# Longer runs of transposes and fewer switches to the attention products, in a hybrid attention and state-space layer

## The chip, the cores and the metric

The kernel runs on one core of one Trainium2 chip. The metric is device time in microseconds (us), the median of three runs. The profile is one further execution; its times are counted from its first instruction.

The engines are named as the profile names them: PE is TensorE (PEld its weight loads), DVE VectorE, ACT ScalarE, POOL GpSimd, SP the queue that issues most of the DMAs.

## The reference

One layer of a decoder trunk, for one sequence of 1024 tokens with 1024 channels, in float32:

```python
mod = c_act @ w_ada[layer] + b_ada[layer]
shift, scale, gate = jnp.split(mod, 3, axis=-1)
h = rms_norm(x, norm_in_gain[layer]) * (1.0 + scale[:, None, :]) + shift[:, None, :]
proj = h @ w_in[layer]
q, k, v, z_attn, xbc, dt_raw, z_ssm = jnp.split(proj, splits, axis=-1)
# stick-breaking attention, 16 heads of 64, in blocks of 128 queries:
z = jnp.einsum("bqhd,bkhd->bhqk", q[:, start:end], k[:, :end]).astype(jnp.float32) * scale
log_one_minus = jnp.where(mask, jax.nn.log_sigmoid(-z), 0.0)
tail = lax.cumsum(log_one_minus, axis=3, reverse=True) - log_one_minus
weights = jnp.exp(jnp.where(mask, log_beta + tail, -jnp.inf))
outs.append(jnp.einsum("bhqk,bkhd->bqhd", weights.astype(v.dtype), v[:, :end]))
# beside it a Mamba-2 head group (16 heads of 64, chunks of 128) on silu(conv(xbc))
y_attn = rms_norm(o, sb_norm_gain[layer]) * jax.nn.silu(z_attn)
y_ssm = rms_norm(y * jax.nn.silu(z_ssm), ssm_norm_gain[layer])
mixed = jnp.concatenate([y_attn, y_ssm], axis=-1) @ w_out[layer]
x = x + gate[:, None, :] * mixed
return rms_norm(x, norm_f_gain)
```

## The kernel before, in words

Every large projection is made of three products of float32r parts (high by high, high by low, low by high), 128x128 weights against 512 columns, summed in one PSUM bank. Splitting a weight piece into its two parts costs DVE (and, early, ACT).

**Front** (lines 424 to 630, up to some 80 us). x, the modulation weights and the first projection weights are loaded. `norm_x` (442) squares a row block on ACT, takes a root on ACT, a reciprocal on DVE, and scales the block on DVE. `ada_mm`, `ada_sum` and `ada_turn` make shift and scale in four rounds from a product on PE and sums on DVE. `turn_x` and `modulate` (500) transpose x on PE and make the high and low parts of h; `mm_h` (517) is the first projection. `fillers` (545) are products with the identity whose result is not used. This stage is in an order written out by hand, on all engines.

**State-space group** (633 to 1220, up to some 315 us): its order is a planner's.

**Attention** (from 1222, some 315 to 940 us): again an order by hand. Heads go in eight pairs. `ROUND` (931) lists the steps of a pair: `scores` (937, "s": PE products of q and k into four banks of `pz`, then sigmoids on ACT, scans and weights on DVE, spread out by `tick`), `turned` (997, "t": the weights of one block of 128 queries are transposed on PE four 128x128 blocks at a time into the single bank of `pt`, and ACT copies the bank back over the weights), and `values` (1013, "v": PE products with v for two blocks, into the single bank of `pv`). The two heads of a pair share PE: scores use half of its rows for each head, values half of its columns. Between these steps `fill` (1285) puts "sides" (`SIDES`, 1189): the projections of q, k, v and the gates for later pairs (`inproj_f`, 295; `inproj_v`, 312), the last one with `turn` (1072), and for pair 7 the state-space half of the output projection (`out_ssm`, 1142). A side gives one step at a time, mostly three matmuls of 512 columns (0.7 us); its sum stands in the two banks of `pj` by turns, and its evacuation (`evac`) reads the bank on ACT (q, k, v) or on ACT and then DVE (gates: `zgate_evac`, 912, `gate_ssm`, 799; output: 1152). `fill(..., True)` after four transposes makes at least one side step, except near a pair's end.

**Tail** (1319 to 1402): the rest of the output projection, in one stretch on PE.

Of the kernel before, what the change touches and what calls it, by code (L numbers as in the profile page):

```python
# [14 lines left out]
P = 128  # L15
# [11 lines left out]
def hybrid_layer_kernel(  # L27
# [156 lines left out]

    h_hi, h_lo = [None] * KT, [None] * KT
# [109 lines left out]
    def inproj_f(col, evac, between=None):  # L295


        wts = take(2) if pinned[0] else split_f(load_f(col))
        for b in range(2):
            ps = bank(pj, "pj")  # L300
            for k in range(KT):
                mm_f(ps, wts, k, b)
                if pinned[0]:
                    ahead()
                    if b and k % 4 == 3:
                        used()
                yield 0.7
            evac(b, ps)
            if between:
                yield between(b)  # L310

    def inproj_v(vc, with_dt, v_tiles, dt_raw, extra=None):
# [19 lines left out]
        for i in range(TB):  # L332
            ps = bank(pj, "pj")
            ts_ = slice(i * P, (i + 1) * P)
            for k in range(KT):
                whi, wlo, ws = wts[k]
                K(T.matmul(ps[:, :n], h_hi[k][:, ts_], whi[:, ws], start=(k == 0), stop=False))  # L337
                K(T.matmul(ps[:, :n], h_hi[k][:, ts_], wlo[:, ws], start=False, stop=False))  # L338
                if i == 0 and extra:
                    extra(ps[:, n:n + TB], k)  # L340
                K(T.matmul(ps[:, :n], h_lo[k][:, ts_], whi[:, ws], start=False, stop=(k == KT - 1)))  # L341
                if not with_dt:
                    ahead()
                    if i == TB - 1 and k % 2:
                        used()
                if k == 3:
                    yield 1.4
            if i == 0 and extra:
                extra(ps[:, n:n + TB], KT)
            for j in range(2):  # L350
                A.copy(v_tiles[j][:, i * P:(i + 1) * P], ps[:, j * P:(j + 1) * P])
            if with_dt:
                A.copy(dt_raw[:, i, :], ps[:, 256:272])
            yield 1.4
# [54 lines left out]
    def split_w4(k):  # L409
# [9 lines left out]
        A.copy(w_hi[k], w_raw[k])  # L419
# [22 lines left out]
    def norm_x(i):  # L442
        junk = mk(op, "om", [P, 1028], bufs=2)
        A.activation(junk[:, :S], xt[i], AF.Square, accum_out=ssq[:, i:i + 1])
        A.activation(rstd[:, i:i + 1], ssq[:, i:i + 1], AF.Sqrt, scale=1.0 / D, bias=eps_t[:, 0:1])
        V.reciprocal(rstd[:, i:i + 1], rstd[:, i:i + 1])
        V.tensor_scalar_mul(xt[i], xt[i], rstd[:, i:i + 1])
# [52 lines left out]
    def modulate(k, hb, ptt=None, c0=0, c1=HALF, full_v=False):  # L500
        ptt = turn_x(k, hb) if ptt is None else ptt
# [11 lines left out]
        V.tensor_tensor(h_lo[k][:, sl], hf, h_hi[k][:, sl].bitcast(F32), op=ALU.subtract)  # L513

    us = []
# [76 lines left out]
    for c_ in range(1, 4):  # L592
# [8 lines left out]
        if c_ == 3:  # L601
            split_lo(6)
        ada_add(c_, ada_turn(c_))
        mm_h(k + 1, 0, range(cut, 4), *cs)
        if c_ < 3:
            ada_mm(c_ + 1)

            mid = (0, 0, 1, 3)[c_ + 1]
            ada_sum(c_ + 1, range(4, 4 + mid - 1), False)
            split_lo(k + 2), split_lo(k + 3)  # L610
# [12 lines left out]
    modulate(1, 1, full_v=True)  # L623
# [175 lines left out]
    def gate_ssm(j):  # L799
# [10 lines left out]
        yield from inproj_f(C_ZS + j * P, evac)  # L810
# [111 lines left out]
    def zgate(p):  # L922
        yield from inproj_f(C_Z + p * P, zgate_evac(p))
# [10 lines left out]
    tiles, pav = {}, {}  # L934
    seq = {"made": 0, "scanned": [], "weights": set()}

    def scores(p, g):
# [5 lines left out]
        for i in {i for i, _, _ in GROUPS[g]}:  # L943
            if i % 2 == 1:
                tiles[p, i // 2] = [duo(), duo()]
        oms = [mk(op, "om", [P, 1028], bufs=2), mk(sp, "bc", [P, S], bufs=4)]
        parts = []
        for i, c0, cw_ in GROUPS[g]:
            zs = [bank(pz, "pz") for _ in range(2)]
            mw = max(cw_, 256)  # L950

            for n, (a, k_) in enumerate(((qh, kh), (qh, kl), (ql, kh))):
                for e in range(2):
                    r = slice(64 * e, 64 * e + 64)
                    K(T.matmul(zs[e][:, :mw], a[r, i * P:(i + 1) * P], k_[r, c0:c0 + mw],  # L955
                               start=(n == 0), stop=(n == 2)))
            parts.append((i, c0, cw_, zs))
        off = {}
        for i, _, _, _ in parts:
            off.setdefault(i, 0 if i == g else 512)  # L960

        def sigmoids(i, c0, cw_, z, e):
            W = (i + 1) * P
            last = c0 + cw_ == W
            be, om = tiles[p, i // 2][e][:, i % 2], oms[e][:, off[i] + c0:off[i] + c0 + cw_]
# [16 lines left out]
        def weights(i, e):  # L982
            W = (i + 1) * P
            be, om = tiles[p, i // 2][e][:, i % 2], oms[e][:, off[i]:off[i] + W]
# [12 lines left out]
    def turned(p, i):  # L997

        for e in range(2):
            if (p, i, e) not in seq["weights"]:  # L1000
                flush("A", lambda: (p, i, e) in seq["weights"] or not late["A"])
                flush("V", lambda: (p, i, e) in seq["weights"])
            be = tiles[p, i // 2][e][:, i % 2]
            for j0 in range(0, i + 1, 4):
                j1 = min(i + 1, j0 + 4)
                ptt = bank(pt, "pt")
                for j in range(j0, j1):
                    K(T.transpose(ptt[:, (j - j0) * P:(j - j0 + 1) * P], be[:, j * P:(j + 1) * P], ident))  # L1008
                A.copy(be[:, j0 * P:j1 * P], ptt[:, :(j1 - j0) * P])
                tick(0.11 * (j1 - j0))  # L1010
                fill(0.5 + 0.1 * (j1 - j0), True)

    def values(p, i0):
        tl, hb, q0 = tiles.pop((p, i0 // 2)), i0 // 4, i0 % 4
        if q0 == 2:
            pav[p] = bank(pv, "pv")
        for j in range(i0 + 2):
            u = int(j > i0)
            for e in range(2):
                K(T.matmul(pav[p][64 * e:64 * e + 64, (q0 + u) * P:(q0 + 2) * P],  # L1020
                           vs[p][:, j * P + 64 * e:j * P + 64 * e + 64],
                           tl[e][:, u:2, j * P:(j + 1) * P], start=(j == 0), stop=(j > i0)))
        if q0 == 2:
            return
# [6 lines left out]
        else:  # L1031
            sq = mk(sp, "th", [P, S], bufs=1)
            A.activation(sq[:, sl], pav[p], AF.Square)
            V.tensor_tensor(sq_a[:, sl], sq_a[:, sl], sq[:, sl], op=ALU.add)
        V.tensor_tensor(zgs[p][:, sl], pav[p], zgs[p][:, sl], op=ALU.mult)
        if hb == 0:
            after(3.0, lambda: (SP.dma_start(y_d[p], zgs[p]), stored.add(p)))
        tick(0.2 * i0 + 0.4)


    def gate_row(b):
        gate = row["sum"][:, b * HALF:(b + 1) * HALF]
        pg = bank(pj, "pj")
# [4 lines left out]
    def outproj(w_h, w_l, evac, first=None):  # L1048

        yt = take(2)  # L1050
        for b in range(2):
            ps = first if first is not None and b == 0 else bank(pj, "pj")
            sl = slice(b * HALF, (b + 1) * HALF)
            for k in range(KT):
# [5 lines left out]
                if b and k % 4 == 3:  # L1060
                    used()
                yield 0.7
            evac(sl, ps)
# [8 lines left out]
    def turn():  # L1072


        wts = take(2)
        pss = [bank(pj, "pj") for _ in range(2)]
# [57 lines left out]
        RATE["V"] = 0.8  # L1134

# [6 lines left out]
    def out_ssm():  # L1142
# [6 lines left out]
        for i in range(TB):  # L1149
            t3 = []  # L1150

            def evac(sl, ps):
                if not t3:
# [37 lines left out]
    COST = {"z": 11.2, "g": 11.2, "q": 22.4, "v": 22.4, "t": 11.3, "o": 36.0}  # L1191
# [42 lines left out]

    def side_step():
# [4 lines left out]
    def count(what, i):  # L1240
        if what == "s":
            return 4.0
        if what == "v":
# [24 lines left out]
    def back(k):  # L1268
# [12 lines left out]
        for n in range(2):  # L1281
            after(2.0, lambda n=n: load_a(k + n, raw[:, n]))
            after(8.0 + 2.0 * n, lambda n=n: split_a(k + n, lambda: place(n)))
# [9 lines left out]
    for p in range(9):  # L1293
        for what, i, before in ROUND:
# [4 lines left out]
            elif what == "t":  # L1299
                turned(p + before, i)  # L1300
            else:
                while p not in box:
                    side_step()
                scores(p, i)
                fill(4.0)
            if (p, what, i) == (6, "s", 1):
# [7 lines left out]
            if (p, what, i) == (7, "s", 1):  # L1314
                front()
            if p == 8 and what == "v":
                back(4 if i else 6)
# [113 lines left out]
```

## Time and profile before

| | us |
|---|---|
| median of 3 runs | 1072.83 (1072.72 to 1073.05) |
| the profiled execution | 1072.53 |
| its span, first to last instruction | 1070.8 |
| PE busy | 1052.9 (98%) |
| DVE busy | 766.2 (72%) |
| ACT busy | 535.6 (50%) |

The busy time of PE counts an instruction from its start to its modelled end, and matmuls overlap, so what PE loses between two kinds of work stands in the distances of the starts rather than as idle time. A float32 matmul stands in the profile as two instructions, one for each pass.

### The profile page before, as it was taken

What the parts mean: (1) busy time and instruction counts of PE and PEld (TensorE: products, weight loads), DVE (VectorE), ACT (ScalarE), POOL (GpSimd) and SP (SyncE); (2) the same over time, 40 slices, a digit from 0 to 9 for tenths busy, and PEclk for the clock granted to TensorE, in tenths of its full rate; (3) what the DMA queues carried; (4) which work ended last, traced back from release to release, by engine and by line L of the source; (5) the groups of instructions that cost most, each with busy time, mean ns of one, the idle gap of its engine ahead of it and who ended that gap; (6) DMA issues with size and microseconds to landing.
All of it is one profiled execution on the core that took longest, in us unless ns stands there. A gap on an engine that the chain in (4) does not pass through costs nothing.

```text
span 1070.8 us, 16251 instructions
## 1 busy us (share of the span) xinstructions
PE 1052.9 (98%) x6323; PEld 836.3 (78%) x6323; DVE 766.2 (72%) x1333; ACT 535.6 (50%) x1163; POOL 2.9 (0%) x23
## 2 busy tenths in 40 slices
PE   7999999999999999999999999999999999999997
PEld 5789887777878777798777887778876777688886
DVE  4838879988848765844977658969387789664554
ACT  5655497676433454554645446546465664420111
POOL 0000000000000000000000000000000000000000
PEclk9999999999999999999999999999999999999999
DMA  9610332233202220201321102311011522555432
GB/s 349 225 41 23 99 107 85 70 96 128 70 20 60 89 78 22 60 20 40 89 60 40 50 21 79 79 40 41 21 50 50 187 88 90 193 186 195 165 108 78
DMA packets 91559, 96.14 MB, mean 90 GB/s; under 512 B 5998, under 2 KB 75994, under 8 KB 91484
## 3 DMA queue, kind: packets, MB, share of 16 engines
q1 hardware_dynamic: 88828, 86.45, 25.8%
q10 hardware_dynamic: 2656, 8.67, 2.3%
q8 instruction: 49, 0.80, 0.3%
q14 instruction: 26, 0.21, 0.1%
HBM read 78.26 MB, written 16.84 MB: 89 GB/s over the span
## 4 chain that ended last, share of the span: by engine, by line
PE 96%; ACT 1%; DMA 1%; DVE 1%; issue 0%; SPq 0%; DVEq 0%; ACTq 0%
PE pj L292 41%; PE pj L1058 15%; PE pt L1008 7%; PE pv L1020 6%; PE pz L955 6%; PE pz L528 4%; PE pj L337 3%; PE pj L341 3%; PE pj L338 3%; PE pz L774 2%; PE pv L788 1%; PE pz L779 1%; PE pj L1380 1%; PE pz L761 1%; PE pj L1123 1%; PE pz L1058 1%
## 5 line engine op out<-in xcount | busy, mean ns | idle before, releaser
L292 PE MATMUL pj<-hh,whi 128*128 128x512 f32 x544 | 225.9, 415 | 0.3 <-ACT th L62 0.3
L292 PE MATMUL pj<-hh,wlo 128*128 128x512 f32 x544 | 214.5, 394 | 0.0
L292 PE MATMUL pj<-hl,whi 128*128 128x512 f32 x544 | 212.7, 391 | 0.0
L62 ACT COPY be<-pt 128x512 f32<-128x512 f32 (+1 forms) x192 | 92.4, 481 | 136.7 <-PE pt L1008 134.4
L292 PEld LDWEIGHTS pj<-hh,whi 128*128 128x128 f32 x544 | 102.5, 188 | 25.3 <-issue 6.3
L292 PEld LDWEIGHTS pj<-hh,wlo 128*128 128x128 f32 x544 | 102.1, 188 | 22.9 <-issue 0.7
L292 PEld LDWEIGHTS pj<-hl,whi 128*128 128x128 f32 x544 | 102.7, 189 | 16.8 <-issue 0.5
L62 ACT ACTIVATE be<-pz 128x512 f32<-128x512 f32 (+3 forms) x192 | 100.9, 526 | 0.0
L1008 PE MATMUL pt<-ident,be 128*128 128x128 f32 x576 | 97.6, 278 | 1.8 <-ACT be L62 1.6
L1008 PEld LDWEIGHTS pt<-ident,be 128*128 128x128 f32 x576 | 67.6, 140 | 38.6 <-ACT be L62 29.0
L62 DVE TENSOR_TENSOR wlo<-raw,whi 128x512 fp32r<-128x512 f32 (+1 forms) x109 | 75.3, 691 | 22.9 <-ACT whi L62 15.9
L62 ACT ACTIVATE om<-pz 128x512 f32<-128x512 f32 (+2 forms) x96 | 47.5, 495 | 75.6 <-PE pz L955 74.8
L62 DVE TENSOR_TENSOR_SCAN om<-om,ident 128x128 f32<-128x128 f32 x64 | 26.8, 419 | 65.9 <-ACT om L62 65.6
L62 DVE TENSOR_TENSOR_SCAN om<-om 128x896 f32<-128x896 f32 (+6 forms) x56 | 71.9, 1285 | 2.0
L62 DVE TENSOR_TENSOR_SCAN bc<-bc 128x896 f32<-128x896 f32 (+6 forms) x56 | 71.9, 1285 | 2.0
L1020 PE MATMUL pv<-be,v 128*64 128x256 f32 (+1 forms) x640 | 69.3, 363 | 0.0
L62 DVE TENSOR_TENSOR be<-be,bc 128x1023 f32<-128x1023 f32 (+4 forms) x78 | 65.3, 838 | 2.4
L337 PE MATMUL pj<-whi,hh 128*128 128x256 f32 (+1 forms) x224 | 66.4, 296 | 0.0
L1020 PEld LDWEIGHTS pv<-be,v 128*64 128x64 f32 x640 | 43.1, 136 | 28.7 <-issue 8.3
L955 PE MATMUL pz<-big,big 64*128 64x384 f32 (+2 forms) x576 | 65.3, 357 | 0.2 <-DVE big L62 0.2
L341 PE MATMUL pj<-whi,hl 128*128 128x256 f32 (+1 forms) x224 | 64.4, 288 | 0.0
L338 PE MATMUL pj<-wlo,hh 128*128 128x256 f32 (+1 forms) x224 | 63.6, 284 | 0.0
(287 smaller groups left out, 1988.4 us busy)
## 6 DMA issues: line engine op xcount, KB each, us to landing
raw<-in_w_in_dram SPq DMA_DIRECT2D x98, 256.0 KB, 2.8
be<-acT_d ACTq DMA_DIRECT2D x16, 512.0 KB, 3.9
big<-in_x_dram SPq DMA_DIRECT2D x10, 512.0 KB, 4.6
aw<-in_w_ada_dram SPq DMA_DIRECT2D x16, 256.0 KB, 5.6
u_d<-big SPq DMA_DIRECT2D x8, 512.0 KB, 3.1
y_d<-bc SPq DMA_DIRECT2D x8, 512.0 KB, 2.6
raw<-in_w_ada_dram SPq DMA_DIRECT2D x16, 256.0 KB, 2.6
raw<-u_d SPq DMA_DIRECT2D x16, 256.0 KB, 2.8
```

The source lines that it names most:

```text
L62: return lambda *args, **kw: K(op(*args, **kw))
L292: K(T.matmul(ps, w[:, ws], h[:, b * HALF:(b + 1) * HALF], start=(k == 0 and n == 0), stop=(k == KT - 1 and n == 2)))
L337: K(T.matmul(ps[:, :n], h_hi[k][:, ts_], whi[:, ws], start=(k == 0), stop=False))
L338: K(T.matmul(ps[:, :n], h_hi[k][:, ts_], wlo[:, ws], start=False, stop=False))
L341: K(T.matmul(ps[:, :n], h_lo[k][:, ts_], whi[:, ws], start=False, stop=(k == KT - 1)))
L528: K(T.matmul(acc[f][:, c0:c1], w[:, f * P:(f + 1) * P], h[:, sl], start=(k == 0 and n == 0 and c0 == 0), stop=(k == KT - 1 and n == 2)))
L761: K(T.transpose(px[:, j * P:(j + 1) * P], xs[4 * g + j][:, ts_], ident))
L774: K(T.matmul(po, xd[:, 0, h, :], m[:, h, :], start=True, stop=(ch == 0)))
L955: K(T.matmul(zs[e][:, :mw], a[r, i * P:(i + 1) * P], k_[r, c0:c0 + mw], start=(n == 0), stop=(n == 2)))
L1008: K(T.transpose(ptt[:, (j - j0) * P:(j - j0 + 1) * P], be[:, j * P:(j + 1) * P], ident))
L1020: K(T.matmul(pav[p][64 * e:64 * e + 64, (q0 + u) * P:(q0 + 2) * P], vs[p][:, j * P + 64 * e:j * P + 64 * e + 64], tl[e][:, u:2, j * P:(j + ...
L1058: K(T.matmul(ps, y[:, ks], w(k, b), start=(k == 0 and n == 0), stop=(k == KT - 1 and n == 2)))
```

## The change

What it does, in six parts:

1. `turned` takes up to two banks of transposes in one run (up to eight 128x128 blocks), the first in `pt`, the second in one of the two `pj` banks; where four blocks or fewer are left for both heads, both go into one bank. Before a run of more than four blocks it makes side steps until the running projection has between 1.3 and 3.6 us left (2.2 where `slow` is set, for projections that DVE evacuates), by `left`, which each side now keeps. While `turn` holds both `pj` banks, a run has one bank.
2. `values` come in two runs a pair instead of four: blocks 6 and 4 one behind the other, 2 and 0 one behind the other. The score group of blocks 1 and 0 is gone; block 1 goes with block 5 and block 0 with block 4, in banks that these leave half empty. So a pair has five score groups, not six. The matmuls are the same, but for the cut of block 5.
3. Blocks 2 and 3 have tiles of their own (`bs`); blocks 1 and 0 lie in the tiles of 5 and 4.
4. The front: the norms are cut into parts and interleaved anew, more of `modulate` is on DVE, one split moves to DVE, three fillers go, `split_lo` comes ahead of `ada_add`, and the loads of x blocks 4 to 7 come ahead of the seven small tables (`late_loads`).
5. `gate_row` uses `pt`, not `pj`; the output projection's `evac` is written ahead of its last `yield`; in `values` the product with the gate comes ahead of the sum of squares.
6. The order near the end: pair 7's first scores wait in the order for the first bank of the output projection; `front`, `back` and the cost of side "o" are set anew; `dynamic_dma_scratch_size=8192`.

The diff, cut:

```diff
-    def inproj_f(col, evac, between=None):
+    def inproj_f(col, evac, between=None, by_v=False):
...
+                left[0], slow[0] = 0.7 * (KT - 1 - k), by_v
                 yield 0.7
...
     load_w4(6), load_w4(7)
-    late_loads()
     for i in range(4, TB):
         load_x(i)
+    late_loads()
...
     fillers(3)
+    norm_sq(1)
+    split_w4(0, V)
+    norm_rt(1)
     pa = ada_turn(0)
-    norm_x(1)
+    norm_by(1, 0, 256)
     ada_add(0, pa)
+    fillers(1)
+    turn_pair(1)
     fillers(4)
-    turn_pair(1)
-    split_w4(0)
-    norm_x(2)
+    norm_sq(2)
...
     split_lo(0)
-    modulate(0, 0, pts[0], *half[0])
+    norm_by(1, 256)
+    modulate(0, 0, pts[0], *half[0], full_v=True)
+    norm_rt(2)
     split_w4(1)
     split_lo(1)
-    modulate(1, 0, pts[1], *half[0])
-    fillers(4)
+    modulate(1, 0, pts[1], *half[0], full_v=True)
+    norm_by(2, 0, 256)
+    norm_sq(3), norm_rt(3)
+    norm_by(3, 0, 256)
     mm_h(0, 0, range(4), *half[0])
+    mm_h(1, 0, range(4), *half[0])
     turn_pair(2)
-    mm_h(1, 0, range(4), *half[0])
-    norm_x(3)
+    turn_pair(3)
     ada_mm(1)
-    turn_pair(3)
+    norm_by(2, 256), norm_by(3, 256)
...
-    norm_x(4)
-    modulate(6, 0, pts[0], full_v=True)
-    split_lo(7)
-    modulate(7, 0, pts[1], full_v=True)
-    norm_x(5), norm_x(6), norm_x(7)
+    norm_sq(4), norm_rt(4), norm_sq(5), norm_rt(5)
+    for f in (h_full, h_low):
+        f(6, 0, pts[0]), f(7, 0, pts[1])
+        if f is h_full:
+            norm_by(4), norm_by(5)
+            split_lo(7)
+    norm_sq(6), norm_rt(6), norm_sq(7), norm_rt(7)
+    norm_by(6, 0, 256), norm_by(7, 0, 256)
     mm_h(6, 0)
-    mm_h(7, 0)
+    mm_h(7, 0, (0, 1))
     modulate(0, 1, full_v=True)
+    norm_by(6, 256), norm_by(7, 256)
+    mm_h(7, 0, (2, 3))
...
-    GROUPS = {7: ((7, 0, 512), (7, 512, 512)), 6: ((6, 0, 512), (6, 512, 384)),
-              5: ((5, 0, 384), (5, 384, 384)), 4: ((4, 0, 384), (4, 384, 256)),
-              3: ((3, 0, 512), (2, 0, 384)), 1: ((1, 0, 256), (0, 0, 128))}
+    GROUPS = {7: ((7, 0, 512, 0, 0), (7, 512, 512, 1, 0)), 6: ((6, 0, 512, 0, 0), (6, 512, 384, 1, 0)),
+              5: ((5, 0, 512, 0, 0), (5, 512, 256, 1, 0), (1, 0, 256, 1, 256)),
+              4: ((4, 0, 384, 0, 0), (4, 384, 256, 1, 0), (0, 0, 128, 1, 256)),
+              3: ((3, 0, 512, 0, 0), (2, 0, 384, 1, 0))}
-    ROUND = (("v", 2, -1), ("s", 7, 0), ("t", 1, -1), ("t", 0, -1), ("s", 6, 0), ("v", 0, -1), ("s", 5, 0),
-             ("t", 7, 0), ("s", 4, 0), ("t", 6, 0), ("v", 6, 0), ("s", 3, 0), ("t", 5, 0), ("t", 4, 0),
-             ("v", 4, 0), ("s", 1, 0), ("t", 3, 0), ("t", 2, 0))
+    ROUND = (("s", 7, 0), ("t", 3, -1), ("t", 2, -1), ("v", 2, -1), ("v", 0, -1), ("s", 6, 0), ("t", 7, 0),
+             ("s", 5, 0), ("t", 6, 0), ("s", 4, 0), ("t", 5, 0), ("t", 1, 0), ("s", 3, 0), ("t", 4, 0),
+             ("t", 0, 0), ("f", 0, 0), ("v", 6, 0), ("v", 4, 0))
...
     def turned(p, i):
+        banks = [(e, j0, min(i + 1, j0 + 4)) for e in range(2) for j0 in range(0, i + 1, 4)]
+        while banks:
+            wide = sum(b[2] - b[1] for b in banks[:2]) > 4
+            while wide and side_left() and left[0] >= 0.0 and not 1.3 < left[0] < (2.2 if slow[0] else 3.6):
+                side_step()
+            n = 1 if wide and left[0] < 0.0 else 2
+            go, banks = banks[:n], banks[n:]
...
+            room, used_, copies = bank(pt, "pt"), 0, []
+            for e, j0, j1 in go:
...
+                if used_ + j1 - j0 > 4:
+                    room, used_ = bank(pj, "pj"), 0
...
+            for to, from_ in copies:
+                A.copy(to, from_)
+            tick(0.11 * sum(j1 - j0 for _, j0, j1 in go))
+            fill(sum(0.5 + 0.1 * (j1 - j0) for _, j0, j1 in go), True)
     def values(p, i0):
...
+        if i0 in (6, 2):
+            while side_left() and clock[0] < free_at[0]:
+                side_step()
             pav[p] = bank(pv, "pv")
...
     def gate_row(b):
-        pg = bank(pj, "pj")
+        pg = bank(pt, "pt")
...
+    def side_left():
+        return done[0] < len(SIDES) - 0.2
...
-        if least and done[0] >= upto[0] and done[0] % 1.0 < 0.93:
+        if least and done[0] >= upto[0]:
             side_step()
```

## Rows read from the trace of the kernel before

**Rows 1.** The page: busy time, and the chain that ended last by engine.
```profile
PE   1052.9 (98%) x6323; PEld 836.3 (78%) x6323; DVE 766.2 (72%) x1333; ACT 535.6 (50%) x1163; POOL 2.9 (0%) x23
...
PE 96%; ACT 1%; DMA 1%; DVE 1%; issue 0%; SPq 0%; DVEq 0%; ACTq 0%
```

**Rows 2.** PE in order of time: start, us, engine, line, out<-in, shape, count.
```profile
650.90 0.27 PE L1008 MATMUL pt<-ident,be 128*128 128x128 f32 x1
650.92 0.47 PE L292 MATMUL pj<-hh,whi 128*128 128x512 f32 x1
651.24 0.39 PE L292 MATMUL pj<-hl,whi 128*128 128x512 f32 x1
651.47 0.40 PE L292 MATMUL pj<-hh,wlo 128*128 128x512 f32 x1
651.79 1.49 PE L955 MATMUL pz<-big,big 64*128 64x512 f32 x12
653.21 0.50 PE L292 MATMUL pj<-hh,whi 128*128 128x512 f32 x1
653.55 0.39 PE L292 MATMUL pj<-hl,whi 128*128 128x512 f32 x1
```

**Rows 3.** PE in order of time, 657.2 to 660.
```profile
657.21 0.39 PE L292 MATMUL pj<-hh,wlo 128*128 128x512 f32 x1
657.52 0.87 PE L1020 MATMUL pv<-be,v 128*64 128x256 f32 x8
658.33 1.32 PE L955 MATMUL pz<-big,big 64*128 64x384 f32 x12
659.57 0.50 PE L292 MATMUL pj<-hh,whi 128*128 128x512 f32 x1
659.91 0.39 PE L292 MATMUL pj<-hl,whi 128*128 128x512 f32 x1
```

**Rows 4.** The chain that ended last, two pieces of it: start, us, what.
```profile
680.26 3.39 PE pv L1020 x32
...
698.68 2.53 PE pv L1020 x24
```

**Rows 5.** PE in order of time: two runs of transposes, three matmuls between them.
```profile
665.07 0.66 PE L1008 MATMUL pt<-ident,be 128*128 128x128 f32 x4
...
666.40 0.66 PE L1008 MATMUL pt<-ident,be 128*128 128x128 f32 x4
```

**Rows 6.** The page's groups: count | busy us, mean ns | idle before, releaser.
```profile
L62 ACT COPY be<-pt 128x512 f32<-128x512 f32 (+1 forms) x192 | 92.4, 481 | 136.7 <-PE pt L1008 134.4
...
L1008 PEld LDWEIGHTS pt<-ident,be 128*128 128x128 f32 x576 | 67.6, 140 | 38.6 <-ACT be L62 29.0
```

**Rows 7.** PE in order of time: last transpose of a run, ahead of values.
```profile
630.11 0.33 PE L1008 MATMUL pt<-ident,be 128*128 128x128 f32 x1 [0.68 <-ACT be L62]
```

**Rows 8.** Two gate evacuations in order of time, each first on ACT, then DVE.
```profile
656.19 0.69 ACT L62 ACTIVATE bc<-pj 128x512 f32<-128x512 f32 x1
...
660.12 0.74 DVE L62 SCALAR_TENSOR_TENSOR bc<-bc,cols,pj 128x512 f32<-128x512 f32 x1
...
708.94 0.60 ACT L62 ACTIVATE bc<-pj 128x512 f32<-128x512 f32 x1
...
709.57 0.75 DVE L62 SCALAR_TENSOR_TENSOR bc<-bc,cols,pj 128x512 f32<-128x512 f32 x1
```

**Rows 9.** By stretch: us, PE, PEld, DVE, ACT, POOL busy, PEclk, DMA.
```profile
20.00:40.00 20.00, 18.93 (x121) 13.92 (x114) 14.91 (x30) 10.58 (x18) 0.00 (x0) 1.00 0.93 323
40.00:60.00 20.00, 18.68 (x98) 15.08 (x97) 14.05 (x27) 14.50 (x27) 0.90 (x5) 1.00 0.37 123
```

**Rows 10.** Front, all engines in order of time: two starts.
```profile
21.68 0.74 PE L528 MATMUL pz<-hh,whi 128*128 128x256 f32 x4 [0.55 <-ACT hh L62]
...
52.93 0.50 PE L528 MATMUL pz<-hl,whi 128*128 128x512 f32 x1 [0.84 <-DVE hl L62]
```

**Rows 11.** The chain that ended last: the stretch after the attention.
```profile
942.49 110.33 PE pj L1058 x486
```

More of the change, by code (lines that the diff above doesn't have):

```diff
@@ L182, in weave @@
                 live.remove(it)
+    left, slow = [0.0], [False]
     h_hi, h_lo = [None] * KT, [None] * KT
@@ L346, in inproj_v @@
                 if k == 3:
+                    left[0], slow[0] = 1.4, False
                     yield 1.4
@@ L353, in inproj_v @@
                 A.copy(dt_raw[:, i, :], ps[:, 256:272])
+            left[0] = 0.0
             yield 1.4
@@ L418, in split_w4 @@
             w_lo[k] = w_far["lo"][:, k // 2 % 2, k % 2 * HALF:(k % 2 + 1) * HALF]
-        A.copy(w_hi[k], w_raw[k])
+        if eng:
+            eng.tensor_copy(w_hi[k], w_raw[k])
+        else:
+            A.copy(w_hi[k], w_raw[k])
     def split_lo(k):
@@ L942, in scores @@
         seq["made"] += 1
-        for i in {i for i, _, _ in GROUPS[g]}:
-            if i % 2 == 1:
-                tiles[p, i // 2] = [duo(), duo()]
+        if g % 2:
+            tiles[p, g // 2] = [duo() if g > 3 else mk(sp, "bs", [P, 2, HALF], bufs=2) for _ in range(2)]
         oms = [mk(op, "om", [P, 1028], bufs=2), mk(sp, "bc", [P, S], bufs=4)]
         parts = []
-        for i, c0, cw_ in GROUPS[g]:
-            zs = [bank(pz, "pz") for _ in range(2)]
+        zs = [[bank(pz, "pz") for _ in range(2)] for _ in range(2)]
+        for i, c0, cw_, b, z0 in GROUPS[g]:
             mw = max(cw_, 256)
@@ L954, in scores @@
                     r = slice(64 * e, 64 * e + 64)
-                    K(T.matmul(zs[e][:, :mw], a[r, i * P:(i + 1) * P], k_[r, c0:c0 + mw],
+                    K(T.matmul(zs[b][e][:, z0:z0 + mw], a[r, i * P:(i + 1) * P], k_[r, c0:c0 + mw],
                                start=(n == 0), stop=(n == 2)))
[L957 to L960, printed above, removed]
+            parts.append((i, c0, cw_, [z[:, z0:z0 + cw_] for z in zs[b]]))
+        off = {i: 0 if i == g else (g + 1) * P for i, _, _, _ in parts}
         def sigmoids(i, c0, cw_, z, e):
@@ L964, in sigmoids @@
             last = c0 + cw_ == W
-            be, om = tiles[p, i // 2][e][:, i % 2], oms[e][:, off[i] + c0:off[i] + c0 + cw_]
+            tl, x0 = place(p, i)
+            be, om = tl[e][:, i % 2, x0:x0 + W], oms[e][:, off[i] + c0:off[i] + c0 + cw_]
             A.activation(om, z[:, :cw_], AF.Sigmoid, scale=-0.125)
@@ L983, in weights @@
             W = (i + 1) * P
-            be, om = tiles[p, i // 2][e][:, i % 2], oms[e][:, off[i]:off[i] + W]
+            tl, x0 = place(p, i)
+            be, om = tl[e][:, i % 2, x0:x0 + W], oms[e][:, off[i]:off[i] + W]
             V.memset(be[:, W - 1:W], 0.0)
@@ L997, in turned @@
     def turned(p, i):
[L999 to L1006, printed above, removed]
-                for j in range(j0, j1):
[L1008 to L1011, printed above, removed]
+        banks = [(e, j0, min(i + 1, j0 + 4)) for e in range(2) for j0 in range(0, i + 1, 4)]
@@ new lines, in turned @@
+        while banks:
[4 more added lines that the diff above has]
+            go, banks = banks[:n], banks[n:]
+            for e, _, _ in go:
+                if (p, i, e) not in seq["weights"]:
+                    flush("A", lambda: (p, i, e) in seq["weights"] or not late["A"])
+                    flush("V", lambda: (p, i, e) in seq["weights"])
+            room, used_, copies = bank(pt, "pt"), 0, []
+            for e, j0, j1 in go:
+                tl, x0 = place(p, i)
+                be = tl[e][:, i % 2, x0:x0 + (i + 1) * P]
+                if used_ + j1 - j0 > 4:
+                    room, used_ = bank(pj, "pj"), 0
+                for j in range(j0, j1):
+                    K(T.transpose(room[:, (used_ + j - j0) * P:(used_ + j - j0 + 1) * P],
+                                  be[:, j * P:(j + 1) * P], ident))
+                copies.append((be[:, j0 * P:j1 * P], room[:, used_ * P:(used_ + j1 - j0) * P]))
+                used_ += j1 - j0
+            for to, from_ in copies:
+                A.copy(to, from_)
+            tick(0.11 * sum(j1 - j0 for _, j0, j1 in go))
+            fill(sum(0.5 + 0.1 * (j1 - j0) for _, j0, j1 in go), True)
@@ L1061, in outproj @@
                     used()
+                left[0], slow[0] = 0.7 * (KT - 1 - k), True
+                if k == KT - 1:
+                    evac(sl, ps)
                 yield 0.7
-            evac(sl, ps)
     t2_d = dr.tile([TB, P, D], F32, tag="t2_d", name="t2_d")
@@ L1075, in turn @@
         wts = take(2)
+        left[0] = -1.0
         pss = [bank(pj, "pj") for _ in range(2)]
@@ L1134, in turn @@
         RATE["V"] = 0.8
+        left[0] = 0.0
     def split_wout(raw, hi, lo):
@@ L1152, in evac @@
             def evac(sl, ps):
+                hooks["first"] = True
                 if not t3:
@@ L1242, in count @@
             return 4.0
-        if what == "v":
+        if what in "vf":
             return 0.0
@@ L1266, in front, with back @@
                                                      mk(sp, "bc", [P, S], F32R, bufs=4)))
-    def back(k):
+    def back(k, late=0.0):
         raw, hi = duo(), duo(F32R)
@@ L1281, in back @@
         for n in range(2):
-            after(2.0, lambda n=n: load_a(k + n, raw[:, n]))
-            after(8.0 + 2.0 * n, lambda n=n: split_a(k + n, lambda: place(n)))
+            after(2.0 + late, lambda n=n: load_a(k + n, raw[:, n]))
+            after(8.0 + late + 2.0 * n, lambda n=n: split_a(k + n, lambda: place(n)))
     def fill(share, least=False):
         upto[0] += share / PER_PAIR
-        if least and done[0] >= upto[0] and done[0] % 1.0 < 0.93:
+        if least and done[0] >= upto[0]:
             side_step()
@@ L1300, in hybrid_layer_kernel @@
                 turned(p + before, i)
+            elif what == "f":
+                fill(2.0)
             else:
@@ L1303, in hybrid_layer_kernel @@
                     side_step()
+                while (p, i) == (7, 7) and "first" not in hooks:
+                    side_step()
                 scores(p, i)
-                fill(4.0)
-            if (p, what, i) == (6, "s", 1):
+                fill(4.0 if i != 3 else 2.0)
+            if (p, what, i) == (6, "f", 0):
                 while "second" not in hooks:
@@ L1313, in hybrid_layer_kernel @@
                 upto[0] = done[0]
-            if (p, what, i) == (7, "s", 1):
+            if (p, what, i) == (7, "f", 0):
                 front()
-            if p == 8 and what == "v":
-                back(4 if i else 6)
+            if (p, what, i) == (7, "v", 4):
+                back(4, 4.0)
+            if (p, what, i) == (8, "v", 0):
+                back(6)
     def more(us):
```

56 lines of the change are left out of this document (36 added, 20 removed).

## The prediction

> **What bounds the kernel now.** I read the page first: PE is busy 98% of the span, and the chain that ended last runs over PE for 96% [rows 1]. DVE (72%) and ACT (50%) have room. So time falls only where PE itself gets faster, and a busy share of 98% seems to leave nothing. The second view, PE in order of time, shows otherwise, if one reads starts and not busy time. In a plain stretch of a projection one 512-column matmul starts every 0.23 us (651.24 to 651.47) [rows 2]. Where PE changes to another kind of work the starts lie further apart, though the row before still counts as busy. I therefore took the attention (315 to 940 us) apart into detours from the projections and compared each with its own work at the plain pace. Three kinds lose time.
>
> The first is a group of scores. From the last projection start ahead of it to the second start behind it (651.47 to 653.55) it takes 2.08 us [rows 2]. Its work is two projection matmuls (0.46) and six pairs of score matmuls, the two heads of a pair side by side: three of 512 columns (0.23 each) and three of 384 (0.17, by columns), 1.20. That leaves 0.42 us for going there and back. The second is values with a group of scores behind them: 657.21 to 659.91 is 2.70 us [rows 3]. A run of 32 value instructions takes 0.86 more than one of 24 [rows 4], so two pairs of 256 columns are 0.43; the run of 8 has two such and two of half the width, 0.65. Six score pairs of 384 are 1.02, two projection matmuls 0.46. That leaves 0.57. The third is the transposes. One of them and the projection matmul behind it (650.90 to 651.24) take 0.34 [rows 2], that is 0.11 for the transpose: the change to transposes and back costs nothing. But two runs of four with three matmuls between start 1.33 us apart [rows 5], where 4 x 0.11 and 3 x 0.23 make 1.13. The 0.2 is the wait for the only bank of `pt`: ACT has to copy it first, 0.48 us each, 192 times [rows 6]. PE's weight loads for transposes sat idle for 29.0 us in front of such copies, part of it under running matmuls [rows 6].
>
> **The change part by part.** *Values and scores.* By `ROUND` there are 48 score groups, 30 of them straight behind values, 18 alone. After it there are 40 (five for each of eight pairs), 14 of them behind values (two for each pair but the first) and 26 alone; before as after, two value runs end the work without scores. Before: 30 x 0.57 + 18 x 0.42 = 24.7 us. After: 14 x 0.57 + 26 x 0.42 = 18.9. Gain 5.8 us, all on PE and so on the path. The products themselves are the same; block 5 is cut into 512 and 256 columns in place of 384 and 384, the same 768. What no row shows is a value run straight behind another. Its cost lies between nothing (same shape, same half of the columns) and what a value run adds of its own, 0.81 - 0.65 = 0.16 [rows 3]; sixteen of these would take 2.6 back. I take nothing, since the shape doesn't change there. Range of the gain 3.2 to 5.8.
>
> The Trainium skill, page TensorEngine Tiling (Array Packing), section Key Properties, says that changing the tiling mode drains TensorE. By it a values-and-scores detour has three changes and a lone group two, so 126 changes become 94, and at 0.21 each (half a lone group's 0.42) the gain would be 6.7 us in place of 5.8. The trace agrees that the loss sits at the changes and not in the length of a run.
>
> *Transposes.* Of the 188 runs of transposes in the attention, 59 waited for the copy (the first at 413.3 us, the last at 930.6), mostly 0.1 or 0.2 as in [rows 5], together 11.4 us by their starts. Two more stand straight ahead of values, 0.84 late each (idle 0.68 [rows 7]), 1.7 us. So 13.1 us of waits are on the path. Afterwards a pair has ten runs of two banks (two each for blocks 7, 6, 5, 4, one each for 3 and 2) and two small ones. A wide run takes 8 x 0.11 = 0.88 and at least one side step follows, 0.69: the next run starts 1.57 or more behind it, and the bank of `pt` was free for the next run after 1.33 [rows 5]. So the old wait goes. What is late next is the second bank, one of the two in which the projections stand. Two things have to be over. The projection before must have left it: on ACT alone two copies of 0.48 [rows 6], and the run comes at the earliest three steps (2.07 us) behind; on ACT and DVE the gate at 656.19 was out at 660.86, 4.7 us after ACT began, the one at 708.94 after 1.4 [rows 8], and the run comes five steps behind (3.45 us), or only three where the projection now running is of q or k, since `slow` tells of the running one and not of the one that left the bank. And the next projection must not be held: the second copy ends about 1.33 + 0.48 = 1.81 us after the run's start, the bank is wanted after 0.88 + 2 x 0.69 = 2.26. This holds by 0.45 as long as ACT, 50% busy, isn't behind. So some runs will wait for DVE. The bounds are no wait at all and one of 4.7 - 2.07 = 2.6 us on each. Seven first banks of q follow a gate; at about 0.4 for these and 0.03 for the other 73 wide runs it is 5 us, nearer to the short end because a score group or values lie between in many cases. Gain 13.1 - 5.0 = 8.1 us; range 0 to 13.1, and what lies below 0 is a rival (Slower). The side steps that the wide runs ask for are moved and not added: their number is that of the projections.
>
> *The bank evacuation order, `gate_row`, tiles `bs`, the scratch size.* These move no work to PE; ACT's 192 copies stay 192 [rows 6]. I take nothing for them. If they cost, it is as DVE or ACT work coming late, which is in the range above.
>
> *The front.* Between 20 and 60 us PE is idle for 1.07 + 1.32 us [rows 9], with waits such as 0.55 for ACT's high part and 0.84 for DVE's low part [rows 10]. The new order brings the first sums one to two us earlier (half a norm instead of a whole one ahead of the transposes, less on ACT ahead of the high parts), and three fillers go. DVE gets a split and two more halves of `modulate`, and six more, shorter norm instructions, and PE waits for it when they are late. The seven small tables on SP's queue now stand behind the four x blocks; they are wanted only at the end of the stage. From nothing lost beyond what idle time is there I bound it by 2.4 us gain and 1 us loss, and take 1.3.
>
> *The end.* Behind the attention PE runs 110 us without a gap [rows 11], with the state-space output first. The new places of `front` and `back` and the later values of blocks 2 and 0 of the last pair are hidden by it; were this cover gone, each us that they are late would count. I take 0.
>
> Sum: 5.8 + 8.1 + 1.3 = 15.2 us. The profiled execution took 1072.5 us, its span 1070.8; the median of the runs is 1072.8, 0.3 above. 1072.5 - 15.2 = 1057.3, and I give 1057.5.
>
> **The rivals.** *Waits as before* (0.20): the wide runs wait for the projections' banks as much as the old ones waited for `pt`, so 13.1 us come back in new places. For it: DVE lets go of a gate's bank after 4.7 us in [rows 8]. Against: 1.4 us in the other. Time: 1072.5 - 5.8 - 1.3 = 1065.4. *All waits go* (0.14): DVE is never late where a wide run stands, and the front gains its idle time. 1072.5 - 5.8 - 13.1 - 2.4 = 1051.2. *Slower* (0.08): every wide run stalls PE, in-order as it is, for the second bank. 80 wide runs; what the rest of the change can give is 5.8 + 13.1 + 1.3 = 20.2 us, so it decides from a mean wait of 0.25 us a run; at 0.4 it is 1072.5 - 20.2 + 32 = 1084. For it: the bank is wanted by three parties, and the gate at 660.12 shows DVE busy with other things first [rows 8]. Against: the order asks for a distance of five steps behind most gates.
>
> The page PSUM — Partial Sum Buffer, section PSUM bank collisions raise a hardware error, of the Trainium skill says that no two engines may access one bank's quadrant at once, so PE may not write while DVE still reads. That is the mechanism of this rival, and the trace agrees as far as the copies of `pt` go; no row shows how often it would strike in `pj`.
>
> *The change doesn't do what it says* (0.04): wide runs fall apart into single banks where `left` is below zero (only the 11 us of `turn`), and values don't stand together. `ROUND` speaks against it: 6 and 4, 2 and 0 follow each other with no side step written between. Time: about 1071.
>
> **How the numbers follow.** The forecast has 0.54, for 1053 to 1062. The range takes in the better case and the waits as before, 1050 to 1067; above it are the slower case and the one without effect, 0.12, and a little of the others. About 0.2% (2 us) is what a measurement of this kernel can tell from no change. Faster by more than that: 0.54 + 0.20 + 0.14 = 0.88; within it 0.04; slower 0.08.
>
> **What would show it.** Right: 40 score groups, of which 14 straight behind values, each detour still at 0.42 and 0.57; runs of eight transposes 0.88 long, followed by projection starts at 0.23; few idle rows of PE in front of transposes. Wrong: PE rows with idle time before the fifth transpose of a run, released by DVE's gate instructions, or before the first matmul of a projection's bank, released by ACT's copies; a second value run that starts late; PE idle between 20 and 60 us grown beyond 2.4 us, released by DVE.

## The result, and the profile after

The changed kernel takes 1063.2 us (median of four runs, 1063.0 to 1063.5) against 1072.9 beside it: ratio 0.991, 95% interval 0.990 to 0.992. The profiled execution took 1063.0 us, and its span is 1061.3. So 9.7 us went, where 15.2 were forecast: inside the range, but outside the 1053 to 1062 of the forecast itself, and nearer to the rival *Waits as before* (1065.4) than to 1057.5.

The page of the kernel after, busy time and the chain that ended last; they answer to [rows 1]:

```profile
PE 1039.0 (98%) x6317; PEld 844.2 (80%) x6317; DVE 768.0 (72%) x1339; ACT 528.6 (50%) x1162; POOL 2.6 (0%) x23
...
PE 86%; DVE 8%; ACT 2%; issue 2%; DMA 1%; ACTq 0%; DVEq 0%; SPq 0%
```

PE's busy share is the same 98%, which again tells nothing. The chain does: it ran over PE for 96% of the span, now for 86%, and DVE, which had 1%, has 8%. DVE does hardly more work than before (768.0 us for 766.2). What changed is that PE now waits for it. The view of PE's waits in the attention, 311 to 925 us (engine, tile, line, released by; us in total, times, longest; the name behind the releasing engine is the tile that it wrote), names the places:

```profile
PE pj L1066 <- DVE bc L62: 3.0, 4, 1.0
PE pj L1066 <- DVE v L62: 1.4, 1, 1.4
PE pj L1066 <- DVE th L62: 1.3, 2, 0.9
PE pj L1066 <- DVE be L62: 1.1, 1, 1.1
PE pz L1003 <- ACT be L62: 0.9, 1, 0.9
PE pt L1066 <- ACT be L62: 0.5, 1, 0.5
```

L1066 is the transpose. All of its waits but one are now in `pj`, the second bank of a run that takes two (a wide run), and DVE ends them; one of 0.5 us is left at `pt`. One of them in PE's order of time (start, us, line, out<-in, shape, count, idle before and its releaser), with the chain over the same stretch:

```profile
513.51 0.39 PE L295 MATMUL pj<-hh,wlo 128*128 128x512 f32 x1
513.74 0.60 PE L1066 MATMUL pt<-ident,be 128*128 128x128 f32 x4
515.31 0.66 PE L1066 MATMUL pj<-ident,be 128*128 128x128 f32 x4 [0.97 <-DVE bc L62]
515.72 0.47 PE L295 MATMUL pj<-hh,whi 128*128 128x512 f32 x1
```

```profile
511.27 0.43 DVE om L62
511.71 0.02 issue
511.73 1.82 DVE om L62
513.55 0.33 DVE whi L62
513.88 0.02 issue
513.90 0.69 DVE wlo L62
514.60 0.67 DVE bc L62
515.26 0.04 issue
515.31 0.66 PE pj L1066 x4
```

The first four transposes start at 513.74, the fifth 1.57 later instead of 0.44. DVE comes to the gate's bank only at some 514.6: a scan of 1.82 us and the split of a weight piece (0.33 and 0.69) stand ahead of it in DVE's order.

For the rest I took the attention apart as in the prediction, each detour against its own work at the plain pace, by starts. Each cell is the number of detours and the us lost in them, that is, how much later than at the plain pace the projection starts again:

| | before | after |
|---|---|---|
| scores alone | 18: 8.1 | 27: 13.2 |
| values and scores | 28: 16.9 | 13: 8.3 |
| values alone, or with transposes | 2: 0.7 | 3: 1.2 |
| transposes, then values and scores | 2: 2.9 | – |
| transposes | 186: 12.7 | 97: 11.1 |
| last product of the front, start (us) | 77.5 | 75.2 |

Counting the two mixed detours of before as 1.2 for values and scores and 1.7 for transposes, the changes of work fell from 27.0 to 22.7 us and the transposes from 14.4 to 11.1; the front gave 2.3. That is 9.9; the spans differ by 9.5, and the 0.4 too much is spread over the rest.

Of f2_later_runs below one execution, the profiled one, was disturbed (2652.5 us); it is left out, and f2_again is the same kernel traced again.

### The profile page after: what moved, and what is told of

It reads as the page before. It is cut to its first block, busy times and chain, and to the rows that moved or that the text cites. A ratio compares the mean times of both kernels' runs of the same rounds, so it can differ in the third digit from the quotient of the medians.

```text
span 1061.3 us, 16252 instructions
## 1 busy us (share of the span) xinstructions
PE 1039.0 (98%) x6317; PEld 844.2 (80%) x6317; DVE 768.0 (72%) x1339; ACT 528.6 (50%) x1162; POOL 2.6 (0%) x23
## 4 chain that ended last, share of the span: by engine, by line
PE 86%; DVE 8%; ACT 2%; issue 2%; DMA 1%; ACTq 0%; DVEq 0%; SPq 0%
PE pj L295 35%; PE pj L1125 13%; PE pv L1084 6%; PE pz L1003 5%; PE pz L553 3%; PE pt L1066 3%; PE pj L345 3%; PE pj L341 3%; PE pj L342 3%; DVE om L62 2%; PE pj L1066 2%; DVE bc L62 2%; PE pz L815 1%; PE pv L829 1%; PE pz L820 1%
## 5 line engine op out<-in xcount | busy, mean ns | idle before, releaser
L295 PE MATMUL pj<-hh,whi 128*128 128x512 f32 x544 | 222.2, 408 | 0.0
L295 PEld LDWEIGHTS pj<-hh,wlo 128*128 128x128 f32 x544 | 102.1, 188 | 22.7 <-issue 0.7
L62 ACT COPY be<-pt 128x512 f32<-128x512 f32 (+2 forms) x98 | 47.1, 499 | 82.7 <-PE pt L1066 79.7
L62 ACT ACTIVATE be<-pz 128x255 f32<-128x255 f32 (+5 forms) x160 | 84.6, 531 | 0.0
L62 ACT ACTIVATE om<-pz 128x512 f32<-128x512 f32 (+1 forms) x96 | 48.0, 500 | 36.1 <-PE pz L1003 36.1
L1003 PE MATMUL pz<-big,big 64*128 64x512 f32 (+2 forms) x576 | 63.5, 354 | 1.1 <-ACT be L62 0.9
L62 ACT ACTIVATE th<-v 128x1024 f32<-128x1024 f32 (+2 forms) x9 | 8.5, 943 | 103.7 <-DVE v L62 103.7
L1003 PEld LDWEIGHTS pz<-big,big 64*128 64x128 f32 x576 | 46.2, 184 | 17.3 <-issue 10.2
L62 DVE TENSOR_TENSOR be<-be,bc 128x1024 f32<-128x1024 f32 (+6 forms) x62 | 55.4, 894 | 1.3
L295 PE MATMUL pj<-hh,st 128*128 128x512 f32 x160 | 55.4, 399 | 0.0
L62 ACT ACTIVATE bc<-pz 128x512 f32<-128x512 f32 (+1 forms) x96 | 53.7, 559 | 0.0
```

The costliest lines, as they stand in the source:

```text
L62: return lambda *args, **kw: K(op(*args, **kw))
L295: K(T.matmul(ps, w[:, ws], h[:, b * HALF:(b + 1) * HALF], start=(k == 0 and n == 0), stop=(k == KT - 1 and n == 2)))
L1003: K(T.matmul(zs[b][e][:, z0:z0 + mw], a[r, i * P:(i + 1) * P], k_[r, c0:c0 + mw], start=(n == 0), stop=(n == 2)))
```

## The experiments

**e1_one_bank**: the changed kernel, but every run of transposes takes one bank.

```diff
-            while wide and side_left() and left[0] >= 0.0 and not 1.3 < left[0] < (2.2 if slow[0] else 3.6):
-                side_step()
-            n = 1 if wide and left[0] < 0.0 else 2
+            n = 1
```

> The changed kernel with every run of transposes in one bank of pt again (and without the side steps that a wide run asks for); order of the pair, fewer switches and new front stay. Theory (late DVE): the wide runs took away the waits for pt, 13.1 us in the kernel before, and got 8.8 us of other waits for them, for banks that DVE had not left; so this kernel loses the difference and the shorter waits come back: 1065 to 1067 against 1063.2 of the change. Rival (wide runs give nothing, the gain is all switches and front): 1063.2, within 0.5. Second rival (wide runs cost more than they give): 1061 or less.

Measured: 1067.1 us (1066.9 to 1067.7), ratio to before 0.995 [0.993, 0.996], just above the 1065 to 1067 expected. The wide runs are worth 3.9 us here, not 8.1. The waits for the copy out of `pt` are back, now also for the gate rows, which the change had moved into that bank (PE's waits, 311 to 945 us; L1109 is the gate rows' product):

```profile
PE pt L1064 <- ACT be L62: 2.0, 5, 1.0
PE pt L1109 <- ACT be L62: 1.4, 2, 0.7
```

**e2_old_front**: the changed kernel with the front in the old order (`norm_x` whole, one round of sums after the other, the small tables ahead of the x blocks).

```diff
-    norm_sq(1)
-    split_w4(0, V)
-    norm_rt(1)
     pa = ada_turn(0)
-    norm_by(1, 0, 256)
+    norm_x(1)
     ada_add(0, pa)
...
```

> The changed kernel with the front of the kernel before (order by hand up to some 77 us and the order of its loads). Theory: PE has no slack behind the front, so the 2.3 us by which the front ended earlier come back in full: 1065.5. Rival: what the front gains is lost again at a later wait on DVE or a transfer: 1063.2 to 1064.

Measured: 1065.7 us (1065.2 to 1066.1), 2.5 more than the change; the last product of the front starts at 77.4 us again, and the attention loses 35.6 us, about as in the change (35.9; the gate rows' products, some 2 us, are counted in here, and the table above leaves them out). So the front is worth some 2.3 us and nothing of it is given back later. The stretches 20 to 40 and 40 to 60 us of the change (us, then busy time of PE, PEld, DVE, ACT, POOL; PEclk, DMA) answer to [rows 9]:

```profile
20.00:40.00 20.00, 19.86 (x125) 15.26 (x122) 16.62 (x32) 12.00 (x21) 0.00 (x0) 1.00 1.07 395
40.00:60.00 20.00, 19.63 (x100) 15.72 (x99) 12.21 (x25) 15.10 (x27) 0.64 (x5) 1.00 0.23 53
```

PE's idle time there fell from 1.07 + 1.32 to 0.14 + 0.37, by 1.88. The first 20 us gave the rest.

**e3_act_evac**: the changed kernel, but the banks of gates and output are emptied by ACT into SBUF, with the scale where there is one, and DVE multiplies from there.

```diff
-            V.scalar_tensor_tensor(zg, zg, cols[:, 92 + p:93 + p], ps, op0=ALU.mult, op1=ALU.mult)
+            full = mk(sp, "ev", [P, HALF], bufs=1)
+            A.activation(full, ps, AF.Copy, scale=cols[:, 92 + p:93 + p])
+            V.tensor_tensor(zg, zg, full, op=ALU.mult)
```

The same is done in `gate_ssm` and in the output's `evac`, and the scratch size is 4096 to make room.

> The changed kernel with the banks of the attention's gates and of the state-space output emptied by ACT alone (ACT copies the sum, scaled where it can, to an SBUF tile, and DVE multiplies from there); DVE's instructions stay as many, ACT gets one of 512 columns more for each bank; a scratch size of 4096 makes room for the tile. Theory (late DVE): the waits of wide runs for DVE (nine runs, 8.8 us by their starts) go: 1054 to 1057. Rival (DVE is the pace there): PE runs ahead and waits for DVE at the next transposes or weights instead: 1062 to 1064. If ACT, with more to do, is late in its place: 1060 or so, with waits for ACT.

Measured: 1053.4 us (1052.7 to 1053.9), ratio 0.982 [0.980, 0.983]: 9.9 us faster than the change, and below the 1054 to 1057 expected. The transposes lose 2.3 us instead of 11.1; the score group behind the output's first bank (*The end*, below) gives 1.3 more. The place shown above (it comes earlier now), on PE, ACT and DVE:

```profile
512.11 0.39 PE L295 MATMUL pj<-hh,wlo 128*128 128x512 f32 x1
512.34 0.60 PE L1072 MATMUL pt<-ident,be 128*128 128x128 f32 x4
512.78 0.60 PE L1072 MATMUL pj<-ident,be 128*128 128x128 f32 x4
513.13 0.48 PE L295 MATMUL pj<-hh,whi 128*128 128x512 f32 x1
```

```profile
511.52 0.75 ACT L62 ACTIVATE ev<-pj,cols 128x512 f32<-128x512 f32 x1
...
513.12 0.68 DVE L62 TENSOR_TENSOR bc<-bc,ev 128x512 f32<-128x512 f32 x1
```

DVE's own part still comes behind the scan and the split, at 513.12, but it no longer holds a bank: ACT was out of it at 512.27. The page shows the price and the chain:

```profile
PE 1036.6 (99%) x6317; PEld 844.4 (80%) x6317; DVE 765.7 (73%) x1339; ACT 551.0 (52%) x1202; POOL 2.7 (0%) x23
...
PE 94%; DMA 2%; DVE 2%; ACT 1%; issue 0%; SPq 0%; DVEq 0%; ACTq 0%
```

ACT works 22 us more, beside PE; DVE is relieved of only 2.3 us. So it isn't DVE's amount of work that cost the time, but the place of the emptying in its order. (f1 below shows that the smaller scratch size isn't it: it has the same size, and no such gain.)

**e4_split_values**: the changed kernel with one side step between the two value runs of each pair.

```diff
-ROUND = (("s", 7, 0), ("t", 3, -1), ("t", 2, -1), ("v", 2, -1), ("v", 0, -1), ...
+ROUND = (("s", 7, 0), ("t", 3, -1), ("t", 2, -1), ("v", 2, -1), ("b", 0, -1), ("v", 0, -1), ...
...
-             ("t", 0, 0), ("f", 0, 0), ("v", 6, 0), ("v", 4, 0))
+             ("t", 0, 0), ("f", 0, 0), ("v", 6, 0), ("b", 0, 0), ("v", 4, 0))
```

> The changed kernel with one side step (three matmuls of 512 columns, or half a value block's projection) put between the two value runs, in up to 16 places; no work is added, steps are moved. Theory (the price lies at the change of kind of work): each place adds a detour of its own, 0.37 us: 16 x 0.37 = 5.9, 1069 us. Rival (only what a value run adds of its own counts, 0.16): 2.6, 1065.8. Rival (the fewer switches gave nothing, the gain is elsewhere): 1063.2.

Measured: 1071.2 us (ten runs, 1069.8 to 1074.0). Sixteen value runs now stand alone, each 0.37 to 0.40 late, 6.2 us together: this confirms the price at the changes of work, where 5.9 was expected. Some 2 us came on top, at one place in the output projection:

```profile
855.61 1.19 PE L1003 MATMUL pz<-big,big 64*128 64x512 f32 x7
858.39 0.96 PE L1003 MATMUL pz<-big,big 64*128 64x512 f32 x5 [1.59 <-DVE v L62]
859.28 0.70 PE L1125 MATMUL pj<-woh,st 128*128 128x512 f32 x1
859.78 0.63 PE L1125 MATMUL pj<-wol,st 128*128 128x512 f32 x1
860.21 1.05 PE L1125 MATMUL pj<-woh,st 128*128 128x512 f32 x2
```

The group of scores is 2.7 us late there (1.9 in the change, where it is at 850.3), and behind it PE ran at the lower of its clocks for a while (last section). The five of the ten runs with the highest granted clock have a median of 1070.2, 7.0 above the change, which is the 6.2 and the 0.8 of longer wait.

**f1_one_bank_act**: e1 and e3 together.

> The changed kernel with both of its edits at once: transposes one bank at a time, as in e1, and the gates' and the output's banks emptied by ACT, as in e3. Theory (a late DVE costs time only because a wide run takes its second bank among the projections' banks): with no wide run ACT's emptying buys next to nothing of the transposes' waits, which stay at 12 us as in e1; at most the 2 us that e1 lost where the banks for the gate rows stood waiting and some 1 us at the scores that wait for an output bank. 1065 to 1067.5 us. Rival (emptying by ACT is a gain of its own, since DVE is then quicker with everything): e1's 1067.1 less the 9.9 us that e3 gained on the change, about 1057.

Measured: 1066.5 us (1065.9 to 1067.0), against 1067.1 for e1. With one bank a run, emptying by ACT brings 0.5 us, within what the measurement can tell; transposes alone lose 12.8 us (12.2 in e1), while the score group behind the output's first bank, 1.9 late in e1, is 0.6 late. The four kernels side by side:

| median us | DVE empties | ACT empties |
|---|---|---|
| one bank a run | 1067.1 (e1) | 1066.5 (f1) |
| two banks a run | 1063.2 (the change) | 1053.4 (e3) |

A wide run is worth 13.2 us where its second bank is free and 3.9 where DVE keeps it; 9.3 us is what the late DVE costs the wide runs. The rival of a gain by ACT alone, which wanted about 1057, falls.

**f2_later_runs** and, for its trace, **f2_again**: the changed kernel, DVE empties, but a wide run behind a gate or an output comes six steps behind it, and the job that left the bank decides, not the running one.

```diff
-                left[0], slow[0] = 0.7 * (KT - 1 - k), by_v
+                left[0], slow[0] = 0.7 * (KT - 1 - k), kind[0]
+                if k == KT - 1:
+                    kind[0] = by_v
...
-            while wide and side_left() and left[0] >= 0.0 and not 1.3 < left[0] < (2.2 if slow[0] else 3.6):
+            while wide and side_left() and left[0] >= 0.0 and not 1.3 < left[0] < (1.5 if slow[0] else 3.6):
```

> The changed kernel, DVE emptying its banks as before, but a wide run behind a gate's or an output's bank starts six steps of the job after it (now five), and that rule goes by the job that left the bank, so that the first bank of a query job behind a gate counts too (now three steps). Theory (each wait in the middle of a wide run is what is left of DVE's emptying when the run comes): the waits of 1.20 and 1.21 us behind a gate's last bank go, each of the others falls by the 0.69 us of one step; of 8.8 us some 2.2 stay, 1056 to 1059 us. Rival (the run waits because DVE is behind by as much wherever the run is put, as it is the pace of the attention): 1063 again.

> The kernel of f2_later_runs again, for a trace of its own: three times of it were 1061.7 to 1063.0 us, so next to nothing of the waits went where the theory wanted 1056 to 1059. If DVE's emptying is done before the later runs come, the waits in their middle are gone and the time is lost at another place; if DVE is behind by as much as before (the rival), the same waits stand one step later, some 9 to 10 us of them.

Measured: 1061.7 to 1063.0 us in three runs of the first, 1061.7 and 1062.6 in the second; the median of the five is 1061.8, 1.4 below the change. Neither theory had that time. The trace shows why (f2_again, PE's waits from 311 to 945 us):

```profile
PE pt L1068 <- ACT bs L62: 2.1, 2, 1.0
...
PE pj L1068 <- DVE th L62: 0.7, 1, 0.7
PE pj L1068 <- DVE bs L62: 0.4, 1, 0.4
PE pj L1068 <- DVE be L62: 0.4, 1, 0.4
```

The waits for DVE in `pj` did go, from 6.8 us in the view of the change to 1.5. But the steps that one run waits for are missing in front of the next. At two places the second of two runs now waits at its *first* bank, 1.0 us idle each (1.4 by starts), for ACT's copy of the run before, and a few others lose 0.1 to 0.2. One of the two, on PE, and the chain over the same stretch:

```profile
570.61 0.60 PE L1068 MATMUL pj<-ident,bs 128*128 128x128 f32 x4
570.97 0.47 PE L295 MATMUL pj<-hh,whi 128*128 128x512 f32 x1
571.28 0.39 PE L295 MATMUL pj<-hl,whi 128*128 128x512 f32 x1
571.51 0.40 PE L295 MATMUL pj<-hh,wlo 128*128 128x512 f32 x1
572.93 0.55 PE L1068 MATMUL pt<-ident,bs 128*128 128x128 f32 x3 [1.03 <-ACT bs L62]
```

```profile
569.94 0.49 ACT th L62
570.43 0.50 ACT bc L62
570.93 0.49 ACT be L62
571.42 0.49 ACT bc L62
571.91 0.49 ACT be L62
572.40 0.49 ACT bs L62
```

The run of 570.18 stands three side steps behind a group of scores; in the change the same run stands ten behind it (571.86). So ACT still has that group's sigmoids (`bc`, `be`) in its order and comes to the copy (`bs`) late. It is the same kind of wait as before, with ACT in DVE's place.

The transposes still lose 9.0 us (11.1 in the change). So DVE is not the pace (the waits did not move along with the runs), but this order of the steps has no room to wait for it either.

## Why the prediction came out as it did

**The changes of work: right.** Forecast 24.7 to 18.9 us, a gain of 5.8. Measured 27.0 to 21.2, without the one wait below: 5.8. There were 27 groups alone and 13 behind values where I had counted 26 and 14, and each detour lost some 0.03 to 0.06 more than by the rows I took, on both sides of the difference. A value run straight behind another, which no row showed, was taken as free, with up to 0.16 each: at 506.46 and 508.03 two such runs of the change start 1.57 us apart, where sixteen instructions make 1.51 by [rows 3] and [rows 4]; 0.06. The Trainium skill, page TensorEngine Tiling (Array Packing), section Key Properties, says that each change of the tiling mode drains TensorE. Counted by it over the detours that are there (130 changes before, 99 after), the gain would be 6.5 us, an estimate at the 0.21 of the prediction. The trace agrees within 0.7, and e4's lone value runs, two changes each, come to 0.19 a change; the rows show the price, not a drain.

**The transposes: the mechanism was right, one term mis-sized.** The old waits did go: with the second bank free they are worth 13.2 us (f1 to e3), forecast 13.1. That these agree so well is in part luck: 10.5 of the 13.2 are transposes (12.8 to 2.3), and most of the rest is waits of the gate rows' products in `pt`, which before stood in `pj`. The step that failed is "so it is 5 us" for the new waits. Nine wide runs wait in the middle for DVE, 8.8 us together by their starts (the view lists eight of them, 6.8 us idle), and small ones bring the term to some 9.3 (the difference between 13.2 and 3.9). It failed at a definite place. For the first banks of q behind a gate I had 7 x 0.4 = 2.8; two of them wait, 1.20 and 1.21 us, 2.4: right in sum, by two waits in place of seven. For the other 73 runs I had 0.03 each, 2.2, because five steps (3.45 us) seemed enough; seven of them wait 0.15 to 1.65 us, 6.4 together. My own row said 4.7 us for one gate out of two [rows 8], and I let the short one decide. What I should have asked is what DVE has in its order ahead of the emptying: at 511.73 to 514.60 a scan of 1.82 us and a weight split of 1.02 stand there, which is more than three steps (2.07) and most of five (3.45). The rival *Waits as before* had the mechanism and too high a price; *Slower* would have needed 0.25 us a run over 80 runs, and 9.3 over 80 is 0.12.

**The next projection is not held: right.** In the view of PE's waits no product of a q, k, v or gate projection waits for the copy of a wide run's second bank; one product of the output does, 0.3 us idle (at 903.39). At 515.72 and 516.03 the first two products behind a run are 0.31 apart, where 0.32 was in [rows 2] (650.92 to 651.24).

**The front: right in sign, short in size.** Forecast 1.3, bound 2.4, measured 2.3 (e2 2.5). I had halved what idle time there was, in case DVE's added work came late. It didn't: 1.88 of the 2.39 us of idle time in [rows 9] went, and the first 20 us gave some more.

**The end, taken as 0: a wait that I had not named.** The first sum of the output projection stands, before as after, in one of the four banks of the scores. Before, the next group of scores came 5.5 us behind the sum's last product (858.80 to 864.26) and didn't stop. In the new order of part 6 it comes right behind (850.02 to 850.34), stops in the middle and loses 1.5 us beyond its change of work. In the order of time:

```profile
850.34 1.19 PE L1003 MATMUL pz<-big,big 64*128 64x512 f32 x7
852.47 0.97 PE L1003 MATMUL pz<-big,big 64*128 64x512 f32 x5 [0.94 <-ACT be L62]
```

Two pairs of runs show that it hangs on DVE's emptying: the group is 1.9 us late in the change and in e1, and 0.6 late in e3 and f1, where ACT empties the output's bank (and the gates'). What the rows don't settle is which bank the group waits for. In e4 the same wait ends with DVE's emptying of the output's bank (`v`). In the change the row names ACT's first sigmoids of the group itself, and DVE comes to its emptying only at 852.68, when the group runs again.

Sum by what was measured: 5.8 + 3.3 + 2.3 - 1.5 = 9.9, against 5.8 + 8.1 + 1.3. Parts 3 and 5 of the change were not taken out by themselves in any run; what they give or cost is somewhere in these terms.

## What to carry to other kernels

Where one engine is to write a bank that another must first empty, size the wait by what stands ahead of the emptying in that engine's order, not by the emptying itself or by how busy the engine is on average: DVE, 72% busy, let a run wait up to 1.4 us. Give the emptying to an engine that has nothing long in its order, even if the other then does nearly the same work from SBUF; with the wide runs that was worth as much as the whole change (9.9 us), and without them nothing that could be measured. To put the wide runs off by a step ended most of the waits for DVE and made others, for ACT.

## What the runs showed of the hardware that was not expected

In e4, behind the stretch in which PE had done little, its granted clock fell. By stretch (us, busy time of PE, PEld, DVE, ACT, POOL; PEclk, DMA):

```profile
856.00:858.00 2.00, 0.80 (x7) 0.32 (x3) 2.00 (x4) 1.08 (x2) 0.00 (x0) 1.00 0.00 0
858.00:860.00 2.00, 1.61 (x7) 1.11 (x8) 0.54 (x2) 0.84 (x2) 0.00 (x0) 0.85 0.04 8
860.00:862.00 2.00, 2.00 (x6) 1.52 (x6) 1.97 (x2) 2.00 (x5) 0.00 (x0) 0.50 0.00 0
862.00:864.00 2.00, 2.00 (x9) 1.58 (x8) 1.90 (x4) 0.20 (x1) 0.00 (x0) 0.80 0.00 0
```

0.50 is 1.2 of 2.4 GHz. The products there start 0.43 us apart instead of 0.23 (859.78 to 860.21 above), and some 1.4 us are lost, beside the 2.7 by which the group itself is late. In the change, where the same group is 1.9 us late, no such fall shows (1.00 in every 2 us from 850 to 860). So one late bank can cost about half as much again behind it. The granted clock recorded for each of e4's ten runs goes with their spread: five with a mean of 0.999 took 1069.8 to 1070.7 us, three with 0.997 took 1071.7 to 1072.1, and two with 0.995 took 1073.6 and 1074.0. Where it fell in the others no trace shows.

And in the places shown a bank of 512 columns took ACT 0.75 us with a scale (e3, 511.52) and DVE 0.74 with both factors (the change, 514.51); DVE's product from SBUF took 0.68 (e3, 513.12). To move the emptying relieves DVE of 2.3 us of 768, and gains 9.9 us all the same.
